# Computing 28 column blocks of the modulations on VectorE instead of 7 wide blocks on TensorE

## The chip, the cores and the metric

The program runs on one core of one Trainium2 chip. The metric is the device time of one execution in microseconds (us). The engines are PE (TensorE matmul; PEld is its weight load), DVE (VectorE), ACT (ScalarE), POOL (GpSimd) and SP (SyncE), which here issues the loads.

## What is computed

Two blocks, one behind the other, on 256 tokens of width 1024 in float32. The first block has three recurrences (HGRN2, mLSTM, SSD), three gated branches and a feed-forward with 22 pairs of hidden blocks. The second block has two layers, each with attention over the stream and a context of 256 tokens and a feed-forward. Each layer of the second block is modulated:

```
def modulation(cond, w_ada, b_ada):
    m = jax.nn.silu(cond) @ w_ada + b_ada
    return [t[..., None, :] for t in jnp.split(m, 6, axis=-1)]

for i in range(DEPTH_2):
    sh1, sc1, g1, sh2, sc2, g2 = modulation(c, w_ada[i], b_ada[i])
    csh1, csc1, cg1, csh2, csc2, cg2 = modulation(c_ctx, w_ada[i], b_ada[i])
    h = modulate(rms_norm(x, norm1_g[i]), sh1, sc1)
    ...
    x = x + g1 * (jnp.concatenate([out_a, out_b, out_c], axis=-1) @ w_out[i])
    x = x + g2 * conv_ffn(modulate(rms_norm(x, norm2_g[i]), sh2, sc2), w_up[i], conv_w[i], conv_b[i], w_down[i])
```

`w_ada[i]` is 1024 x 6144 and there are two conditions, so a layer's modulations are a product of two rows with 25 MB of weights. They don't depend on the stream, and can be computed at any time before the place that reads them: columns 0 to 2047 (shift and scale) before the layer's first norm, 2048 to 3071 (the first gate) before its output projection, 3072 to 5119 before its second norm, 5120 to 6143 (the last gate) before the end of its feed-forward.

## The kernel before, in words

Every product of the stream is done with weights on the fly. A weight tile of 128 x 1024 floats (512 KB) is loaded by SP into `raw` (four buffers), ACT casts it to a high part `wh`, DVE subtracts to get the low part `wl` (three buffers each), and PE makes three passes per 128 rows: wh with the high part of the data, wh with the low part, wl with the high part. For 256 tokens a tile is 24 matmuls of 256 columns; they write a bank `psg` (three buffers).

The modulations are made in steps that the function `ada_tick` hands out after every `pace`-th weight tile. There are two ways. `ada_pe` takes 512 columns at a time on PE: a step loads a weight tile of 256 rows x 512 columns into the same `raw`, casts and splits it like any other weight, and makes four matmuls of 512 columns with the conditions as the other operand (`psada`, L541 and L542); four steps make a wide block, and then `finish` turns its two rows into columns with four transposes (`psat`) and two small DVE additions. `ada_dve` takes 128 columns with the columns on the partitions: a 128 x 1024 tile is loaded, and for each condition one DVE instruction multiplies it with the condition's row (`ccb`, on every partition) and sums along the row (L580); a block is two steps. `ada_rows` loads and prepares `ccb` (1 MB, eight activations, eight DVE instructions).

The table `ADA` says who does which columns. Layer 0's 12 wide blocks (48 steps) all go through `ada_pe`: 36 steps during the branches of the first block, 12 in the first block's feed-forward. Layer 1's first 40 blocks of 128 columns go through `ada_dve`, in layer 0's feed-forward (the second feed-forward of the program), with tiles of their own (`araw`, three buffers); its last two wide blocks go through `ada_pe` in layer 1's attention.

Each engine executes its own list in order. A scheduler arranges these lists when the program is built: it moves instructions ahead of others where their operands allow it, so the place of a step in the code is only roughly its place in the lists. `prepare(i)` loads a layer's parameters (`plt`) and derives its small tables on DVE; it needs the columns of that layer's shift and scale.

Of the kernel before, what the change touches and what calls it, by code (L numbers as in the profile page):

```python
# [2 lines left out]

# [25 lines left out]
# columns of the modulations done on the tensor engine, 512 at a time, and on the vector engine, 128  # L29
ADA = ((range(0, 6144, 512), range(0)), (range(5120, 6144, 512), range(0, 5120, 128)))  # L30
# [3 lines left out]
# column offsets of the first block's w_in  # L34
# [4 lines left out]
# rows of the small projections: i gates, f gates, dt  # L39
# [3 lines left out]
def _ws(name, layer, c0, nk=8, r0=0):  # L43
    """[nk*128, 128] block of a weight, rows on partitions, 128 columns."""
    def cut(w):
        return w[name][layer][r0:r0 + nk * 128, c0:c0 + 128].reshape(nk, 128, 128).transpose(1, 0, 2)
    return nk * 128, cut


def _xs(name, layer, c0, half, cols=None):  # L50
    """[512, 256] block: rows on partitions, 256 columns that stream."""
# [7 lines left out]
def _ada(layer, c0, q):  # L59
    """[256, 512] block: rows on partitions, 512 columns."""  # L60
    def cut(w):
        a = w["w_ada_2"][layer][q * 256:(q + 1) * 256, c0:c0 + 512]
        return a.reshape(2, 128, 512).transpose(1, 0, 2)
    return 1024, cut


def _adat(layer, c0):
    """[1024, 128] block: columns on partitions."""
# [19 lines left out]
def _qcols(c):  # L88
    """256 columns of the window attention's queries, heads j and j + 4 side by side."""
# [35 lines left out]
def plan2(layer):  # L125
    p = [(("ada", c0, q), _ada(layer, c0, q)) for c0 in ADA[layer][0] for q in range(4)]
    p += [(("adat", c0), _adat(layer, c0)) for c0 in ADA[layer][1]]
# [21 lines left out]
def _cols(v):  # L149
    """[n*128] -> [128, n]"""  # L150
    return v.reshape(-1, 128).T


def _convc(w):
    """[K, n*128] -> [128, n*K]"""
# [121 lines left out]
class Knobs:  # L277
# [8 lines left out]
    pace3 = 5  # L286
# [13 lines left out]
def tile_two_blocks(ctx: ExitStack, tc: tile.TileContext, xT, ctxT, cst1, cst, cstw, pb1, pl0, pl1, pf0, pf1, pc, pcb, wb, w0, w1, out,  # L300
# [16 lines left out]
    class PS:  # L317
        """PSUM pools of the phase at hand"""

    def psum(**bufs):  # L320
        """Shares out the eight banks: name=number."""
# [38 lines left out]
    ones = const.tile([128, 128], F32, name="ones")  # L360
    V.memset(ones, 1.0)
    onesn = const.tile([128, 128], F32, name="onesn")
# [5 lines left out]
    def bsel(r):  # L368
        """[128, 128]: row r ones; picks and broadcasts one row."""
        return ident[:, r:r + 1].to_broadcast([128, 128])  # L370

# [21 lines left out]
    def gained(dst_h, dst_l, x, g):  # L393
        """x g, split: what the first products after a norm take; 1 / rms is applied to their results"""
# [4 lines left out]
    def mm3(o, w, rhs, nk, late=False, first=True, last=True):  # L399
        """o = W^T x in three passes; late: the low part of x comes last."""  # L400
# [11 lines left out]
    def gemm_ws(ph, key, rhs, n, nk=8, late=False, w=None):  # L412
        """out[128 features, n tokens] = W^T x; rhs(k) gives (high, low)."""
# [6 lines left out]
    def gemm_xs(ph, keys, lhs, toks, evac):  # L420
        """out[128 tokens, 256 features]; lhs(k, t) gives (high, low) of a token tile."""
# [14 lines left out]
    def rsqrt_raw(pool, a, n, tag, bufs, rows=128):  # L436
        """RS * result = 1 / sqrt(a)"""
# [3 lines left out]
        # in two halves, so that neither waits for the step before  # L441
# [13 lines left out]
    def mean_sq(x, scale=None, eps=EPS):  # L455
        """mean of squares + eps, [128 tokens, 2 blocks of them], in PSUM"""
# [20 lines left out]
    def rms_all(a):  # L477
        """[128, 256] on every partition: 1 / (RS sqrt(a)) for tokens on partitions"""
# [19 lines left out]
    # =====================================================================  # L498
    # modulation: silu(c) w + b for both conditions, features on partitions
    # =====================================================================  # L500
# [22 lines left out]
    def ada_pe(li):  # L523
        """512 columns at a time on the tensor engine; both parts of the conditions share a pass."""
# [10 lines left out]
        for c0 in ADA[li][0]:  # L535
            ps = (PS.a or PS.s).tile([128, 512], F32, tag="s", name="psada")
            for q in range(4):
# [7 lines left out]
                if q < 3:  # L545
                    yield
            rows = [Ada.rows.tile([128, 256], F32, tag="arow", name="arow", bufs=2) if Ada.rows is not None else
                    tmp.tile([128, 256], F32, tag="t256", name="arow", bufs=6) for _ in range(2)]
# [11 lines left out]
    def ada_rows(pool):  # L560
        """twice silu(c) of both conditions, on every partition"""
# [9 lines left out]
    def ada_dve(li):  # L571
        """128 columns at a time, on partitions: products summed along the rows"""
        for c0 in ADA[li][1]:
            o, sz = woff[1 + li][("adat", c0)]
            f = c0 // 128
            raw = Ada.pool.tile([128, 1024], F32, tag="araw", name="araw", bufs=Knobs.araw)
            nc.sync.dma_start(out=raw, in_=wsrc[1 + li][o:o + 128 * sz].rearrange("(p f) -> p f", p=128))
            for c in range(2):
                to = Ada.pool.tile([128, 1024], F32, tag="prod", name="prod", bufs=1) if c == 0 else raw
# [4 lines left out]
    def ada_tick():  # L584
        """After each weight tile: now and then a step."""
# [16 lines left out]
    # =====================================================================  # L602
    # convolution, SwiGLU, down projection
    # =====================================================================
    def ffn(ph, pool, halves, xh, xl, cw3, cb, causal, resid, hook=None, mid=None, raw=None):
        """halves: 1 or 2 blocks of 256 tokens. With two, the first columns take the second block first and the
# [1162 lines left out]
```

## Time and profile before

| what | value |
|---|---|
| median of 3 runs | 1767.18 us (1764.59 to 1767.67) |
| profiled execution, first to last instruction | 1767.7 us |
| PE busy | 1738.8 us (98%), PEld 1568.2 us (89%) |
| DVE busy | 1384.8 us (78%) |
| ACT busy | 983.7 us (56%) |
| loads | 273.9 MB read, 156 GB/s over the span |

The profiled execution spans 1767.7 us, which is the time of the longest of the three runs to a tenth; the median lies 0.5 us below. The busy share is an average over stages. Matmuls overlap in the pipeline, so a matmul's duration in a row is longer than what it adds to the time; the distance from one start to the next is what it adds. The stages by time: projections and HGRN2 to about 240 us, mLSTM, SSD and the branches 240 to 560, first feed-forward 560 to 760, layer 0's attention to 1000, its feed-forward 1000 to 1390, layer 1 from there.

### The profile page before, as it was taken

To read this page: it belongs to the slowest core of one execution; us is meant where nothing else is said; L and a number is where in the kernel's file an instruction comes from. 1 tells how busy PE (TensorE), PEld (TensorE's weight loads), DVE (VectorE), ACT (ScalarE), POOL (GpSimd) and SP (SyncE) were. 2 spreads that over 40 slices of the span, in tenths; PEclk is the share of its full clock that TensorE was granted. 3 is DMA by queue.
4 is the path that set the end of the run, shared out by engine and by line. 5 is a ranking of instruction groups with operands and counts; after the bars stand their busy time and mean duration, and the time that the engine had idled before them with its cause. 6 is when DMAs were issued, how large, how long until landed. Compare 5 with 4: busy or idle time off the path is not lost.

```text
span 1767.7 us, 31912 instructions
## 1 busy us (share of the span) xinstructions
PE 1738.8 (98%) x12442; PEld 1568.2 (89%) x12442; DVE 1384.8 (78%) x2716; ACT 983.7 (56%) x1723; POOL 0.2 (0%) x4
## 2 busy tenths in 40 slices
PE   7999999999999999999999999999999999999999
PEld 7999988878888999999878898888888997799999
DVE  7987967557778996877687799999656878788776
ACT  6655645445556865666676564442244556766554
POOL 0000000000000000000000000000000000000000
PEclk8999999999999999999989999999999999999999
DMA  7555445447677666654211356657433543046564
GB/s 233 159 154 152 138 132 157 147 126 222 218 228 228 187 190 221 209 170 139 86 67 47 105 163 189 183 171 232 129 96 107 168 132 120 24 141 195 174 196 132
DMA packets 80502, 276.97 MB, mean 157 GB/s; under 512 B 9056, under 2 KB 13792, under 8 KB 80224
## 3 DMA queue, kind: packets, MB, share of 16 engines
q1 hardware_dynamic: 80352, 274.94, 49.8%
q8 instruction: 98, 1.61, 0.4%
q14 instruction: 52, 0.43, 0.1%
HBM read 273.86 MB, written 1.05 MB: 156 GB/s over the span
## 4 chain that ended last, share of the span: by engine, by line
PE 51%; DVE 3%; ACT 1%; issue 0%; ACTq 0%
PE psg L404 12%; PE psg L407 12%; PE psg L406 11%; PE pso L1574 3%; PE psx L429 2%; PE psx L431 2%; PE psx L430 2%; PE psp L1562 2%; PE psc L1517 1%; PE psc L1519 1%; PE psc L1518 1%; DVE wl L385 0%; ACT Pp L1529 0%; DVE mx L1523 0%; PE psc L1521 0%
## 5 line engine op out<-in xcount | busy, mean ns | idle before, releaser
L383 ACT CAST wh<-raw 128x1024 fp32r<-128x1024 f32 (+1 forms) x475 | 490.9, 1037 | 531.0 <-PE psg L406 423.7
L385 DVE TENSOR_TENSOR wl<-raw,wh 128x1024 fp32r<-128x1024 f32 (+1 forms) x475 | 572.5, 1208 | 206.8 <-ACT wh L383 203.2
L404 PE MATMUL psg<-XH,wh 128*128 128x256 f32 (+1 forms) x1288 | 400.7, 314 | 3.6 <-ACT XH L390 1.9
L407 PE MATMUL psg<-XH,wl 128*128 128x256 f32 (+1 forms) x1288 | 398.8, 312 | 0.3 <-DVE wl L385 0.3
L406 PE MATMUL psg<-XL,wh 128*128 128x256 f32 (+1 forms) x1240 | 387.5, 313 | 0.7 <-DVE XL L1304 0.5
L404 PEld LDWEIGHTS psg<-XH,wh 128*128 128x128 f32 x1288 | 243.0, 189 | 22.0 <-ACT XH L390 2.3
L407 PEld LDWEIGHTS psg<-XH,wl 128*128 128x128 f32 x1288 | 243.3, 189 | 15.9 <-DVE wl L385 1.0
L406 PEld LDWEIGHTS psg<-XL,wh 128*128 128x128 f32 x1240 | 234.5, 189 | 16.1 <-DVE XL L1304 1.1
L404 PE MATMUL psg<-xh,wh 128*128 128x256 f32 x704 | 203.4, 289 | 1.8 <-ACT xh L390 1.3
L406 PE MATMUL psg<-xl,wh 128*128 128x256 f32 x704 | 200.5, 285 | 0.9 <-DVE xl L391 0.9
L407 PE MATMUL psg<-xh,wl 128*128 128x256 f32 x704 | 200.1, 284 | 0.3 <-DVE wl L385 0.3
L404 PE MATMUL psg<-hh,wh 128*128 128x256 f32 (+1 forms) x592 | 179.6, 305 | 0.1
L407 PE MATMUL psg<-hh,wl 128*128 128x256 f32 (+1 forms) x592 | 178.5, 302 | 0.0
L406 PE MATMUL psg<-hl,wh 128*128 128x256 f32 (+1 forms) x592 | 178.5, 302 | 0.0
L404 PEld LDWEIGHTS psg<-xh,wh 128*128 128x128 f32 x704 | 134.9, 192 | 6.0 <-ACT xh L390 1.5
L406 PEld LDWEIGHTS psg<-xl,wh 128*128 128x128 f32 x704 | 135.1, 192 | 2.9 <-DVE xl L391 1.4
L407 PEld LDWEIGHTS psg<-xh,wl 128*128 128x128 f32 x704 | 134.9, 192 | 2.2 <-issue 1.3
L406 PEld LDWEIGHTS psg<-hl,wh 128*128 128x128 f32 x592 | 111.5, 188 | 5.3 <-DVE hl L391 0.2
L404 PEld LDWEIGHTS psg<-hh,wh 128*128 128x128 f32 x592 | 110.9, 188 | 5.9 <-ACT hh L390 0.6
L407 PEld LDWEIGHTS psg<-hh,wl 128*128 128x128 f32 x592 | 111.2, 188 | 5.5
L429 PE MATMUL psx<-wh,XH 128*128 128x256 f32 x384 | 110.0, 287 | 1.1 <-DVE ss L1379 0.5
L430 PE MATMUL psx<-wh,XL 128*128 128x256 f32 x384 | 108.5, 283 | 0.0
(435 smaller groups left out, 3237.8 us busy)
## 6 DMA issues: line engine op xcount, KB each, us to landing
raw<-w SPq DMA_DIRECT2D x254, 512.0 KB, 3.7
raw<-wb SPq DMA_DIRECT2D x197, 512.0 KB, 4.3
araw<-w SPq DMA_DIRECT2D x40, 512.0 KB, 4.2
raw<-w SPq DMA_DIRECT2D x16, 384.0 KB, 3.4
raw<-wb SPq DMA_DIRECT2D x8, 384.0 KB, 3.2
xres<-xT SPq DMA_DIRECT2D x16, 128.0 KB, 3.6
plt<-pl SPq DMA_DIRECT2D x2, 588.0 KB, 5.5
xres<-ctxT SPq DMA_DIRECT2D x8, 128.0 KB, 2.7
```

Of the source, the lines that this page charges most:

```text
L383: S.copy(wh[:, 0:sz], raw[:, 0:sz])
L385: V.tensor_tensor(wl[:, 0:sz], raw[:, 0:sz], wh[:, 0:sz], ALU.subtract)
L404: T.matmul(o, wh[:, k], xh, start=(first and k == 0), stop=False)
L406: T.matmul(o, wh[:, k], xl, start=False, stop=False)
L407: T.matmul(o, wl[:, k], xh, start=False, stop=(last and not late and k == nk - 1))
L429: T.matmul(o, xh, wh[:, k % 4], start=(k == 0), stop=False)
L430: T.matmul(o, xl, wh[:, k % 4], start=False, stop=False)
L431: T.matmul(o, xh, wl[:, k % 4], start=False, stop=(k == 7))
L1517: T.matmul(o, qh, kh, start=True, stop=False)
L1518: T.matmul(o, qh, kl, start=False, stop=False)
L1562: T.transpose(ps[:, b], p[:, b * 128:(b + 1) * 128], ident)
L1574: T.matmul(po[:, i % 4], pt[:, b], v, start=(b == 0), stop=(b == nb - 1))
```

## The change

28 of layer 0's 48 column blocks of 128 go from `ada_pe` to `ada_dve`. Columns 0 to 2559 (20 blocks, `e` = 0) are handed out from the branches on, with tiles from the weights' own four `raw` buffers (`own` false). Columns 2560 to 5119 (5 wide blocks) stay on PE, behind the 20. Columns 5120 to 6143 (8 blocks, `e` = 2) go in front of layer 1's 40 in the second feed-forward, with tiles `araw`. A second `ccb` is loaded and prepared early in the first block. `pace3`, the pace in the first feed-forward, is 3 instead of 5. The first of the two products of a block is written in bfloat16 (`prod`; only the sum is used), and `prod`'s buffer also holds the rows of `finish`. Two small constants shrink, comments are taken out. In the second feed-forward `prepare(1)` comes two hidden blocks later, behind a line that makes sure that 48 steps are done.

```
-ADA = ((range(0, 6144, 512), range(0)), (range(5120, 6144, 512), range(0, 5120, 128)))
+ADA = ((range(0, 2560, 128), range(2560, 5120, 512), range(5120, 6144, 128)),
+       (range(0), range(5120, 6144, 512), range(0, 5120, 128)))
...
-    pace3 = 5
+    pace3 = 3
...
-            rows = [Ada.rows.tile([128, 256], F32, tag="arow", name="arow", bufs=2) if Ada.rows is not None else
-                    tmp.tile([128, 256], F32, tag="t256", name="arow", bufs=6) for _ in range(2)]
+            if Ada.rows is not None:
+                row = Ada.rows.tile([128, 512], F32, tag="prod", name="arow", bufs=1)
+                rows = [row[:, 0:256], row[:, 256:512]]
+            else:
+                rows = [tmp.tile([128, 256], F32, tag="t256", name="arow", bufs=6) for _ in range(2)]
...
-    def ada_dve(li):
+    def ada_dve(li, e, own):
-        for c0 in ADA[li][1]:
+        for c0 in ADA[li][e]:
...
+            if own:
+                o, sz = woff[1 + li][("adat", c0)]
+                raw = Ada.pool.tile([128, 1024], F32, tag="araw", name="araw", bufs=Knobs.araw)
+                nc.sync.dma_start(out=raw, in_=wsrc[1 + li][o:o + 128 * sz].rearrange("(p f) -> p f", p=128))
+            else:
+                raw = weight_raw(1 + li, ("adat", c0))
             for c in range(2):
-                to = Ada.pool.tile([128, 1024], F32, tag="prod", name="prod", bufs=1) if c == 0 else raw
+                to = Ada.pool.tile([128, 1024], BF16, tag="prod", name="prod", bufs=1) if c == 0 else raw
...
     ada_prep()
-    Ada.pace, Ada.steps, Ada.rows = Knobs.pace0, ada_pe(0), p1
+    Ada.pool, Ada.cb = p1, ada_rows(p1)
+    Ada.pace, Ada.steps, Ada.rows = Knobs.pace0, chain(ada_dve(0, 0, False), ada_pe(0)), p1
...
-        ada_steps(max(0, 17 - Ada.done))
+        ada_steps(max(0, 32 - Ada.done))
...
-            Ada.pace, Ada.steps = Knobs.pace2, ada_dve(1)
+            Ada.pace, Ada.steps, Ada.done = Knobs.pace2, chain(ada_dve(0, 2, True), ada_dve(1, 2, True)), 0
 
             def hook(j):
-                if j == 16:
+                if j == 13:
+                    ada_steps(max(0, 16 - Ada.done))
+                if j == 18:
+                    ada_steps(max(0, 48 - Ada.done))
                     LS[1] = prepare(1)
```

The lists of the engines show where the steps fall. First DVE in the branches of the first block, before the change: `wl` is the split of a weight tile, two of the branch's for each of the modulation's, `th` and `mixed` are the branch's own work, `mod0` the end of a wide block.

```order
L385 TENSOR_TENSOR wl_5198<-raw_5194,wh_5196 128x1024
L385 TENSOR_TENSOR wl_5231<-raw_5227,wh_5229 128x1024
L385 TENSOR_TENSOR wl_5263<-raw_5259,wh_5261 128x1024
L1173 SCALAR_TENSOR_TENSOR th_5036<-th_5036,psg_5200 128x256
L1174 TENSOR_TENSOR mixed_603<-mixed_603,th_5036 128x256
L385 TENSOR_TENSOR wl_5282<-raw_5278,wh_5280 128x1024
L385 TENSOR_TENSOR wl_5315<-raw_5311,wh_5313 128x1024
L530 TENSOR_TENSOR mod0_93<-psat_5269,pf0_575 128x8
L385 TENSOR_TENSOR wl_5346<-raw_5342,wh_5344 128x1024
L532 TENSOR_TENSOR mod0_93<-mod0_93,psat_5269 128x8
```

The same place with the change; L590 is the product with its sum (on `prod` for the first condition, on `raw` itself for the second) and the reading of the sum.

```order
L389 TENSOR_TENSOR wl_5091<-raw_5087,wh_5089 128x1024
L1184 SCALAR_TENSOR_TENSOR th_4878<-th_4878,psg_5023 128x256
L1185 TENSOR_TENSOR mixed_629<-mixed_629,th_4878 128x256
L389 TENSOR_TENSOR wl_5124<-raw_5120,wh_5122 128x1024
L590 ISA prod_5220,mod0_93<-raw_5218,ccb_585,pf0_575 128x1024
L590 ISA mod0_93 128x1
L389 TENSOR_TENSOR wl_5158<-raw_5154,wh_5156 128x1024
L590 ISA raw_5218,mod0_93<-raw_5218,ccb_585,pf0_575 128x1024
L590 ISA mod0_93 128x1
L1184 SCALAR_TENSOR_TENSOR th_4948<-th_4948,psg_5093 128x256
L1185 TENSOR_TENSOR mixed_629<-mixed_629,th_4948 128x256
L389 TENSOR_TENSOR wl_5191<-raw_5187,wh_5189 128x1024
```

One split in three is gone; for every four weight tiles two products have come. The tile `raw_5218` is loaded into the buffer that `raw_5087` leaves, so its load starts when `wl_5091` is made, and one more split lies between the two.

The load queue of SP at this place, before the change (`w0` are layer 0's modulations, `wb` the first block's weights).

```order
L376 DMA raw_5893<-w0 128x1024
L376 DMA raw_5909<-wb 128x1024
L376 DMA raw_5942<-wb 128x1024
L376 DMA raw_5974<-w0 128x1024
L376 DMA raw_5993<-wb 128x1024
```

And with the change.

```order
L380 DMA raw_5081<-w0 128x1024
L380 DMA raw_5087<-wb 128x1024
L380 DMA raw_5120<-wb 128x1024
L380 DMA raw_5154<-wb 128x1024
L380 DMA raw_5187<-wb 128x1024
L380 DMA raw_5218<-w0 128x1024
```

Every fifth load is now the modulation's, where it was every third. Of the 20 blocks, 19 stand in DVE's list between the start of the branches and the first feed-forward's first products, the last one a little behind; the 20 steps of `ada_pe` that are left all stand in the first feed-forward or directly behind it.

## Rows read from the trace of the kernel before

**Rows 1.** The page: span, and busy time of two engines.

```profile
span 1767.7 us, 31912 instructions
...
PE 1738.8 (98%) x12442; PEld 1568.2 (89%) x12442; DVE 1384.8 (78%) x2716; ACT 983.7 (56%) x1723; POOL 0.2 (0%) x4
```

**Rows 2.** Busy time by stretch: PE, PEld, DVE, ACT, POOL; granted clock, DMA share, GB/s.

```profile
20.00:100.00 80.00, 76.40 (x612) 74.27 (x611) 69.58 (x136) 54.32 (x91) 0.00 (x0) 0.96 0.56 173
240.00:560.00 320.00, 317.91 (x2299) 270.99 (x2298) 220.44 (x366) 170.14 (x305) 0.00 (x0) 0.99 0.58 181
560.00:600.00 40.00, 35.88 (x283) 33.40 (x283) 36.17 (x89) 27.90 (x50) 0.00 (x0) 1.00 0.62 191
1040.00:1240.00 200.00, 200.00 (x900) 163.56 (x900) 194.50 (x293) 77.96 (x107) 0.00 (x0) 1.00 0.60 185
1240.00:1360.00 120.00, 120.00 (x528) 97.11 (x527) 70.73 (x91) 42.92 (x53) 0.00 (x0) 1.00 0.34 105
```

**Rows 3.** Waits of PE from 240 to 560 us: in total, times, longest.

```profile
PE psada L541 <- ACT wh L383: 1.6, 1, 1.6
```

**Rows 4.** Waits of ACT from 405 to 560 us.

```profile
ACT wh L383 <- PE psg L406: 43.8, 29, 3.5
```

**Rows 5.** Waits of ACT from 1040 to 1240 us.

```profile
ACT wh L383 <- PE psg L406: 103.2, 31, 4.6
```

**Rows 6.** Matmuls of tile psada alone, by stretch: PE busy (count), PEld, ACT.

```profile
240.00:560.00 320.00, 39.82 (x144) 11.98 (x144) 5.52 (x18) 0.99 0.58 181
560.00:600.00 40.00, 2.36 (x8) 0.67 (x8) 0.00 (x0) 1.00 0.62 191
```

**Rows 7.** Timeline of PE around two steps: start, duration, what.

```profile
298.40 0.39 PE L541 MATMUL psada<-wh,ccr 128*4 128x512 f32 x1
...
299.42 0.41 PE L528 MATMUL psat<-ct,arow 4*128 4x4 f32 x4
299.76 0.38 PE L404 MATMUL psg<-xh,wh 128*128 128x256 f32 x1
...
305.47 0.40 PE L541 MATMUL psada<-wh,ccr 128*4 128x512 f32 x1
...
306.40 0.28 PE L404 MATMUL psg<-yh,wh 128*128 128x256 f32 x1
306.52 0.28 PE L406 MATMUL psg<-yl,wh 128*128 128x256 f32 x1
```

**Rows 8.** Timeline of PE at the first feed-forward's start.

```profile
567.24 0.71 PE L482 MATMUL psr<-ct,rcy 128*128 128x128 f32 x4 [1.79 <-DVE rcy L451]
567.88 0.41 PE L528 MATMUL psat<-ct,arow 4*128 4x4 f32 x4
...
582.69 0.40 PE L541 MATMUL psada<-wh,ccr 128*4 128x512 f32 x1
```

**Rows 9.** Timeline of DVE in the same place.

```profile
566.85 0.17 DVE L1248 TENSOR_SCALAR g5n1g<-plt 128x8 f32<-128x8 f32 x1 [2.44 <-DMA plt<-pl]
```

**Rows 10.** Line L580, the product with its sum, and the reading of the sum.

```profile
L580 DVE DVE_READ_ACCUMULATOR2_ANT mod<- x80: 80/83/88, 1046.6 to 1253.6; 128x1 f32 x80
L580 DVE CUSTOM_DVE_ANT_0 prod<-araw,ccb,pf x40: 1273/1278/1283, 1045.4 to 1251.0; 128x1024 f32<-128x1024 f32 x40
```

**Rows 11.** The page's groups: cast and split of weight tiles (busy, mean ns, idle before).

```profile
L383 ACT CAST wh<-raw 128x1024 fp32r<-128x1024 f32 (+1 forms) x475 | 490.9, 1037 | 531.0 <-PE psg L406 423.7
L385 DVE TENSOR_TENSOR wl<-raw,wh 128x1024 fp32r<-128x1024 f32 (+1 forms) x475 | 572.5, 1208 | 206.8 <-ACT wh L383 203.2
```

**Rows 12.** The page's DMA issues: count, size, median us to landing.

```profile
raw<-w SPq DMA_DIRECT2D x254, 512.0 KB, 3.7
```

**Rows 13.** Tile ccb, its DVE instructions.

```profile
L568 DVE SCALAR_TENSOR_TENSOR ccb<-th,ccb x8: 421/422/424, 1041.9 to 1045.1; 128x256 f32<-128x256 f32 x8
```

**Rows 14.** Timeline of SP, 0 to 70 us: start, duration, loads issued.

```profile
21.94 4.26 SPq L494 DMA_DIRECT2D xres<-xT  x8
31.85 17.34 SPq L376 DMA_DIRECT2D raw<-wb  x8
```

More of the change, by code (lines that the diff above doesn't have):

```diff
@@ L2 @@
 from contextlib import ExitStack
+from itertools import chain
 import numpy as np
@@ L125, in plan2 @@
 def plan2(layer):
-    p = [(("ada", c0, q), _ada(layer, c0, q)) for c0 in ADA[layer][0] for q in range(4)]
-    p += [(("adat", c0), _adat(layer, c0)) for c0 in ADA[layer][1]]
+    p = [(("ada", c0, q), _ada(layer, c0, q)) for c0 in ADA[layer][1] for q in range(4)]
+    p += [(("adat", c0), _adat(layer, c0)) for e in (0, 2) for c0 in ADA[layer][e]]
     for h in range(2):
@@ L317, in tile_two_blocks @@
     class PS:
+        pass
     def psum(**bufs):
@@ L359, in tile_two_blocks @@
     ident = C("ident")
-    ones = const.tile([128, 128], F32, name="ones")
+    ones = const.tile([128, 1], F32, name="ones")
     V.memset(ones, 1.0)
-    onesn = const.tile([128, 128], F32, name="onesn")
+    onesn = const.tile([128, 1], F32, name="onesn")
     V.memset(onesn, 1.0 / 1024.0)
@@ L534, in ada_pe @@
         last = None
-        for c0 in ADA[li][0]:
+        for c0 in ADA[li][1]:
             ps = (PS.a or PS.s).tile([128, 512], F32, tag="s", name="psada")
@@ L569, in ada_rows @@
         return t
-    def ada_dve(li):
-        for c0 in ADA[li][1]:
-            o, sz = woff[1 + li][("adat", c0)]
+    def ada_dve(li, e, own):
+        for c0 in ADA[li][e]:
             f = c0 // 128
-            raw = Ada.pool.tile([128, 1024], F32, tag="araw", name="araw", bufs=Knobs.araw)
-            nc.sync.dma_start(out=raw, in_=wsrc[1 + li][o:o + 128 * sz].rearrange("(p f) -> p f", p=128))
+            if own:
[4 more added lines that the diff above has]
+                raw = weight_raw(1 + li, ("adat", c0))
             for c in range(2):
-                to = Ada.pool.tile([128, 1024], F32, tag="prod", name="prod", bufs=1) if c == 0 else raw
+                to = Ada.pool.tile([128, 1024], BF16, tag="prod", name="prod", bufs=1) if c == 0 else raw
                 V.tensor_tensor_reduce(to, raw, Ada.cb[:, c], 0.5, Ada.pf[li]("bada")[:, f:f + 1], ALU.mult, ALU.add,
```

## The prediction

> **What bounds the kernel now.** I read the page first: PE is busy 98% of a span of 1767.7 us, DVE 78% [rows 1]. A share of busy time can mislead, so I went to the stretches in which the change works [rows 2] and asked who waits for whom there. From 240 to 560 us, where 36 of layer 0's 48 modulation steps lie (144 matmuls, four a step [rows 6]), PE is busy 317.9 of 320 us and DVE 220.4; the longest wait of PE in all of it is 1.6 us [rows 3]. The preparation of the weights is the other way round: ACT's casts wait for PE to give a buffer back, 43.8 us in the last 155 us of the stretch [rows 4], and over the whole program 423.7 us [rows 11]. So the weights are ready before PE wants them, and PE alone sets the pace. The one stretch near the change where that fails is the start of the first feed-forward, 560 to 600 us: PE idles 4.1 us [rows 2], 1.8 us of it in front of the norm's broadcast [rows 8], behind a DVE that itself stood 2.4 us for a load of parameters [rows 9].
>
> **What a step on PE is worth.** The timeline gives the distance of starts, which is what counts: a plain step goes from 305.47 to the next weight's first matmul at 306.40, 0.93 us; a step with the transposes of `finish` from 298.40 to 299.76, 1.36 us, so `finish` adds 0.43 us [rows 7]. The four matmuls thus start 0.23 us apart, though each lasts 0.4 us in its row. The Trainium skill ("TensorE: Matmul & The Clock Gate", Back-to-back issue gap) states about 131 ns per matmul of 512 columns in a sustained stream, and 216 ns alone; by the first of these a step would be an estimated 0.52 us and the sum 11 us smaller. The rows show a stream, and neither figure; the trace decides.
>
> **The change, part by part.**
>
> Taken from PE: 7 of 12 wide blocks, 28 steps and 7 finishes: 28 x 0.93 + 7 x 0.43 = 26.0 + 3.0 = 29.0 us. In place it is more movement than that: 36 steps leave 240 to 560 us, and the first feed-forward has 20 steps instead of 12. Not all of it is on the path: two of the old steps (8 matmuls [rows 6]) and one finish (567.88 [rows 8]) lie in the 40 us in which PE idles anyway, and filled holes: 2 x 0.93 + 0.43 = 2.3 us off. That leaves 26.7 us.
>
> Put on DVE: 56 products of 1.28 us and 56 readings of 0.08 us [rows 10], against 28 splits of 1.21 us [rows 11] that go. One product has a bfloat16 output, which no row shows; half of 1.28 us is the floor if the written bytes decided, 1.28 us the ceiling by the nearest row, with the same two float32 inputs; I take 1.28. In the branches, 19 of the 20 blocks come to 19 x 2 x 1.36 = 51.7 us and 36 splits go (43.6 us), so DVE rises from 220.4 us to some 228 us, of the 283 us that the stretch has left when 36 steps and 8 finishes are gone from it (36.9 us). It stays under PE: price 0, while the cover holds.
>
> The wait that this adds: a product needs its tile, whose load starts when a buffer of the weights' ring comes free, one split ahead of it in DVE's list. A load takes 3.7 us [rows 12], and PE goes through a weight tile of 24 matmuls in about 2.8 us (0.12 us from start to start, 306.40 to 306.52 [rows 7]), so DVE will stand about 1 us at the first product. Queued behind it are the next weight's split and the evacuation of the branch's products; PE waits for the first, and through its result buffers for the second. The two products and the wait come to some 3.7 us in which DVE also owes one split; with three buffers the preparation runs up to two tiles (5.6 us) ahead, so most of these stalls end in that lead. Bounds: 0, and 20 blocks x 2.7 us = 54 us if every pair of products stood bare. I take 1 us in all, close to the lower end, because DVE has 55 us of slack there.
>
> The start of the program: a second `ccb` costs 8 DVE instructions of 0.42 us [rows 13], 3.4 us, in a stretch where DVE is busy 69.6 of 80 us and PE already idles 3.6 us [rows 2]. The 1 MB load itself falls into a hole of SP: its issues end at 26 us and the next weight's starts at 31.85 us [rows 14]. Bounds 0 and 3.4 us; I take 1 us, because DVE has 10 us of slack but little lead.
>
> The first feed-forward's start: in DVE's list one pair of products now lies around the last sums of squares, and the parameters' small tables are spread through the norm's chain of short instructions; the standstill of 2.4 us for the parameters [rows 9] is covered by more work ahead of it. Gain up to 2.4 us, loss up to two products, 2.7 us. I take 0.
>
> The second feed-forward: 16 more products and readings, 16 x 1.36 = 21.8 us of DVE, which is busy 194.5 of 200 us from 1040 to 1240 us. PE is busy 200.0 of 200 there all the same, and ACT's casts wait for PE 103.2 us [rows 5]: DVE is full and still ahead. The products come no denser than before, they only end later, and from 1240 to 1360 us DVE has 49 us free [rows 2]. Price 0; without that cover 21.8 us. `prepare(1)` two hidden blocks later moves inside the same cover. The later steps of `ada_pe` in the first feed-forward are counted above: they cost 0.93 us each, wherever PE is full.
>
> Sum: -26.7 + 1 + 1 = -24.7 us, 1767.7 - 24.7 = 1743.0 us for an execution like the profiled one. The median of the runs lies 0.5 us under it: **1742.5 us**.
>
> **Rivals.**
>
> *Part is given back on DVE.* If the ring of four buffers or the products in front of the branches' work expose some 0.5 us for each of 20 blocks, and the start costs its whole 3.4 us, the change gives back 10 to 13 us: about 1752. For it: every stall sits in front of a split; DVE's use there rises from 69% to 81%. Against it: the casts' waits for PE [rows 4].
>
> *PE isn't the bound.* PE's busy time is a sum of overlapping, partly modelled durations, and PEld is busy only 271 of the 320 us [rows 2]. If what really paces the branches were loads or casts, the removed steps would only make room for waits, and the time would stay near 1766. The Trainium skill ("Perfetto Trace Analysis", Identifying the Most-Contended Engine) warns just so: matmul occupancy is no good measure of the distance to the limit, the share of weight loads is. Against it stands the unbroken row of starts through the steps [rows 7] and that one wait of 1.6 us [rows 3].
>
> *Slower: a block as a brake on the weights.* The modulation's tile keeps its ring buffer until its second product is done, and only then can the weight four places on be loaded (3.7 us), cast (1.04 us) and split (1.21 us): 6.0 us in all, against 2.8 us that PE needs for a tile. Bare, that is 3.2 us for each of 20 blocks, 64 us, and a time near 1806. It decides from 1.5 us a block on: then 30 us eat the 26.7 us and 3.5 us more. Against it: the next three tiles are in other buffers, and the lead would have to be gone before.
>
> **How the numbers follow.** The forecast, 1737 to 1748: 0.66. Part given back, 1748 to 1764: 0.20. PE not the bound, within 0.2% (3.5 us, about what a measurement of this kernel can tell from no change): 0.06. Slower through the ring: 0.05. Better than 1737, if the first feed-forward's start also loses its standstill and every step counts (29.0 + 1.6 + 2.4 us: down to 1734): 0.03. The range 1735 to 1756 leaves out the two that end elsewhere and the worse half of the second case, some 0.2 in all. Faster 0.89, same 0.06, slower 0.05.
>
> **What the next profile would show.** Right: 112 matmuls of `psada` fewer, none before the first feed-forward; PE as full from 240 us as before, and the branches ending some 36 us earlier (36.9 less the stalls), of which the first feed-forward gives back about 10 (8 x 0.93 + 0.43 for what it does more, 2.3 for the filled holes); DVE near 81% busy in the branches; waits of DVE for loads there of about 1 us, some 20 times, and hardly any of PE; the second feed-forward as long as before. Wrong: waits of PE for `wl` or `wh` in the branches, by the dozen; PE idle for more than 5 us from 20 to 100 us, or for more than 8 us around the first feed-forward's start; or PE's starts further apart between 1040 and 1360 us.

## The result, and the profile after

The changed kernel takes 1748.74 us (median of 4 runs, 1745.11 to 1749.94); beside it the kernel before takes 1767.43 us (4 runs, 1764.59 to 1768.96). The ratio is 0.9897, with an interval of 0.9879 to 0.9915: faster, as forecast, and inside the range, but 6.2 us above the 1742.5 us named. It lies 0.7 us outside the band of 1737 to 1748 us that the prediction gave to its own case, in the band of its first rival; the traces show that it isn't that rival's mechanism that put it there.

The page of the changed kernel answers to [rows 1].

```profile
span 1746.6 us, 31615 instructions
...
PE 1707.4 (98%) x12302; PEld 1552.8 (89%) x12302; DVE 1415.7 (81%) x2794; ACT 957.2 (55%) x1689; POOL 0.2 (0%) x4
```

PE has 31 us less, DVE 31 us more, and PE's share is 98% again. The next lines are busy time by stretch (columns as in [rows 2]) of the program's start, the branches, the first feed-forward's start and the second feed-forward, to be set against [rows 2].

```profile
20.00:100.00 80.00, 73.27 (x602) 71.51 (x602) 71.95 (x143) 56.09 (x98) 0.00 (x0) 0.99 0.58 180
240.00:525.00 285.00, 281.59 (x2123) 256.15 (x2122) 214.29 (x380) 131.25 (x249) 0.00 (x0) 0.99 0.55 172
525.00:565.00 40.00, 33.56 (x265) 32.75 (x263) 36.51 (x93) 26.47 (x49) 0.00 (x0) 0.96 0.51 162
1020.00:1220.00 200.00, 200.00 (x906) 163.80 (x906) 194.55 (x294) 78.16 (x108) 0.00 (x0) 1.00 0.60 183
```

The matmuls of `psada` alone, by stretch [rows 6]: none is left in the branches, 72 stand in the first feed-forward and 8 behind it.

```profile
240.00:525.00 285.00, 0.00 (x0) 0.00 (x0) 0.00 (x0) 0.99 0.55 172
525.00:746.00 221.00, 19.55 (x72) 6.05 (x72) 2.46 (x8) 0.99 0.67 208
746.00:764.00 18.00, 2.02 (x8) 0.68 (x8) 0.61 (x2) 1.00 0.55 181
```

PE is still full in the branches (281.6 of 285 us) and in the second feed-forward (200.0 of 200), with DVE at 75% in the one and 97% in the other. PE's idle time has grown at the start (6.7 of 80 us, 3.6 before [rows 2]) and at the first feed-forward's start (6.4 of 40 us).

Where the time went shows when the same matmul starts in the two traces:

| matmul | before, us | after, us | after less before |
|---|---|---|---|
| first `psl` (HGRN2) | 55.14 | 56.61 | +1.47 |
| first `psF` (mLSTM) | 242.09 | 244.21 | +2.12 |
| first `psw` (mLSTM) | 246.21 | 249.47 | +3.26 |
| last product on `mh` (end of the branches) | 560.18 | 527.34 | -32.84 |
| first product on `XH` (first feed-forward) | 572.92 | 539.74 | -33.18 |
| last product on `hh` there | 769.60 | 746.82 | -22.78 |
| 120th `psx` (layer 0's projections) | 787.46 | 769.33 | -18.13 |
| first product on `hh` of the second feed-forward | 1189.05 | 1170.48 | -18.57 |
| last one of its first pass | 1267.23 | 1248.64 | -18.59 |
| end | 1767.7 | 1746.6 | -21.1 |

Each column is one execution. The first 260 matmuls of PE are the same in all kernels, yet the 261st starts between 46.8 and 50.3 us in the twelve traces of this document, at 49.95 us in the kernel before and at 50.28 us here; so 0.3 us of the first rows is not the change's.

From the first `psF` to the last product on `mh` both kernels make the same 1727 matmuls into `psg`, and the kernel before 36 steps and 8 finishes more. This stretch takes 283.1 us instead of 318.1: the branches give 35.0 us. The first feed-forward takes back 10.4, and another 4.7 us go where nothing was expected, between the last product of the first feed-forward and layer 0's projections. The waits of PE in the branches, 240 to 525 us, come to 3.4 us (engine, line, waited for; total, times, longest):

```profile
PE psr L1143 <- DVE rqy L455: 1.5, 1, 1.5
PE psg L410 <- DVE ml L395: 1.0, 2, 0.7
PE psg L408 <- ACT mh L394: 0.7, 1, 0.7
PE psg L411 <- DVE wl L389: 0.2, 1, 0.2
```

The products themselves, line L590 (ns min/median/max, first and last start, forms), and what DVE waited for before them (us, times):

```profile
L590 DVE CUSTOM_DVE_ANT_0 prod<-raw,ccb,pf x20: 1267/1284/1286, 235.6 to 557.6; 128x1024 bf16<-128x1024 f32 x20
L590 DVE CUSTOM_DVE_ANT_0 raw<-raw,ccb,pf x20: 1264/1280/1286, 236.9 to 563.6; 128x1024 f32<-128x1024 f32 x20
...
  DMA raw<-w: 21.5, 14
```

A bfloat16 output changes nothing (1284 against 1280 ns). DVE stands 14 times for a tile, 1.5 us on average. Only 0.2 us of PE's waiting is for a split (`wl`), but the longest wait, 1.5 us for `rqy`, comes behind two products in a norm of the branches, the first of which stood 2.56 us for its tile:

```profile
452.75 1.28 DVE L590 CUSTOM_DVE_ANT_0 prod<-raw,ccb,pf 128x1024 bf16<-128x1024 f32 x1 [2.56 <-DMA raw<-w]
...
453.96 0.41 DVE L1124 TENSOR_SCALAR ms<-psn 4x256 f32<-4x256 f32 x1
454.29 1.26 DVE L590 CUSTOM_DVE_ANT_0 raw<-raw,ccb,pf 128x1024 f32<-128x1024 f32 x1
...
455.50 0.34 DVE L448 TENSOR_SCALAR rqy<-ms 4x128 int32<-4x128 int32 x2
```

In the kernel before `rqy` starts 0.45 us behind `ms` (473.84 and 474.29 us), here 1.54 us, and PE doesn't wait for it there.

**The turn.** The lists of ACT, DVE and PE where the first feed-forward ends (start, duration, instruction, idle time before it and its releaser):

```profile
749.13 0.61 ACT L557 COPY arow<-psada 4x256 f32<-4x256 f32 x2
749.65 2.50 ACT L465 ACTIVATE sq<-xres,pb1t 128x256 f32<-128x256 f32 x6
752.06 2.92 ACT L387 CAST wh<-raw 128x1024 fp32r<-128x1024 f32 x3
```

```profile
747.13 0.42 DVE L1327 TENSOR_TENSOR xres<-psg,xres 128x256 f32<-128x256 f32 x1 [0.27 <-PE psg L411]
...
756.11 1.23 DVE L389 TENSOR_TENSOR wl<-raw,wh 128x1024 fp32r<-128x1024 f32 x1
757.26 0.15 DVE L455 SCALAR_TENSOR_TENSOR rcy<-rct,rcy 128x2 f32<-128x2 f32 x1
757.33 1.22 DVE L389 TENSOR_TENSOR wl<-raw,wh 128x1024 fp32r<-128x1024 f32 x1
758.46 0.15 DVE L451 TENSOR_TENSOR rct<-rcy 128x2 f32<-128x2 f32 x1
758.53 1.22 DVE L389 TENSOR_TENSOR wl<-raw,wh 128x1024 fp32r<-128x1024 f32 x1
...
762.18 1.27 DVE L1313 SCALAR_TENSOR_TENSOR h<-xres,gx,rr 128x256 f32<-128x256 f32 x3
```

```profile
748.56 0.40 PE L546 MATMUL psada<-wl,ccr 128*2 128x512 f32 x1
...
757.39 0.39 PE L435 MATMUL psx<-wl,XH 128*128 128x256 f32 x1 [1.48 <-DVE wl L389]
```

The last two steps of `ada_pe` are handed out behind the feed-forward, and PE makes them from 746.94 us on. They leave layer 0 one weight tile ahead; the next three casts then lie behind the squares of the norm and the copies of `arow` on ACT, come all at once at 752.06, and their three splits stand between the norm's tiny instructions. From the last residual (747.13) to the first `h` (762.18) it is 15.05 us. In the kernel before it was 10.3 us:

```profile
769.92 0.42 DVE L1316 TENSOR_TENSOR xres<-psg,xres 128x256 f32<-128x256 f32 x1 [0.23 <-PE psg L407]
...
780.24 0.88 DVE L1302 SCALAR_TENSOR_TENSOR h<-xres,gx,rr 128x256 f32<-128x256 f32 x2
```

**The first feed-forward's start.** PE there, by the timeline:

```profile
539.74 0.73 PE L408 MATMUL psg<-XH,wh 128*128 128x256 f32 x3 [2.92 <-ACT XH L394]
540.79 0.41 PE L408 MATMUL psg<-XH,wh 128*128 128x256 f32 x1
541.43 0.41 PE L408 MATMUL psg<-XH,wh 128*128 128x256 f32 x1
```

And busy time and clock behind it, by stretch:

```profile
539.70:543.50 3.80, 3.76 (x18) 3.72 (x19) 3.80 (x12) 2.28 (x7) 0.00 (x0) 0.55 0.31 113
543.50:550.00 6.50, 6.50 (x56) 6.42 (x54) 5.11 (x19) 4.95 (x10) 0.00 (x0) 1.00 0.00 0
```

Behind the norm's broadcast PE is now empty for 2.9 us; before, a `finish` [rows 8] and the rest of a product stood there, and the wait was 1.9 us. For 3.8 us after it the granted clock is 0.55, nearly all of it the lower of the two levels (1.2 instead of 2.4 GHz): starts 0.21 us apart instead of 0.12. Before, the granted clock was 1.00 in the same place [rows 2]. That doesn't make the fall the change's alone: in the run with the second feed-forward's part alone (below), PE's wait for `XH` is 1.86 us, as in the kernel before, and there the clock fell all the same:

```profile
569.31:573.22 3.91, 3.91 (x18) 3.76 (x19) 3.91 (x12) 2.75 (x8) 0.00 (x0) 0.56 0.24 96
```

A little later PE waits 1.9 us for `ag` (551.98 us), where the kernel before doesn't wait.

### The profile page after: what moved, and what is told of

It is laid out like the page before. It is cut to its first block, busy times and chain, and to the rows that moved or that the text cites. A ratio compares the mean times of both kernels' runs of the same rounds, so it can differ in the third digit from the quotient of the medians.

```text
span 1746.6 us, 31615 instructions
## 1 busy us (share of the span) xinstructions
PE 1707.4 (98%) x12302; PEld 1552.8 (89%) x12302; DVE 1415.7 (81%) x2794; ACT 957.2 (55%) x1689; POOL 0.2 (0%) x4
## 4 chain that ended last, share of the span: by engine, by line
PE 50%; DVE 4%; ACT 1%; DMA 1%; issue 1%; ACTq 0%; DVEq 0%; SPq 0%
PE psg L408 12%; PE psg L411 12%; PE psg L410 11%; PE pso L1585 2%; PE psx L433 2%; PE psx L435 2%; PE psx L434 2%; PE psp L1573 1%; PE psc L1528 1%; DVE wl L389 1%; PE psc L1530 1%; DVE mx L1534 1%; PE psc L1529 1%; ACT Pp L1540 0%; ACT wh L387 0%
## 5 line engine op out<-in xcount | busy, mean ns | idle before, releaser
L387 ACT CAST wh<-raw 128x1024 fp32r<-128x1024 f32 (+1 forms) x447 | 462.1, 1037 | 506.0 <-PE psg L410 413.2
L389 DVE TENSOR_TENSOR wl<-raw,wh 128x1024 fp32r<-128x1024 f32 (+1 forms) x447 | 538.3, 1207 | 151.2 <-ACT wh L387 148.7
L435 PE MATMUL psx<-wl,XH 128*128 128x256 f32 x384 | 108.1, 283 | 1.5 <-DVE wl L389 1.5
```

The source lines that it names most:

```text
L387: S.copy(wh[:, 0:sz], raw[:, 0:sz])
L389: V.tensor_tensor(wl[:, 0:sz], raw[:, 0:sz], wh[:, 0:sz], ALU.subtract)
L435: T.matmul(o, xh, wl[:, k % 4], start=False, stop=(k == 7))
```

## The experiments

Ten runs follow, nine of them of new kernels. The ratio is to the kernel before, run on the same chip. The last column is worked out from each trace: from the start of the first feed-forward's last product on `hh` to the start of the 120th `psx`.

| run | median, us | ratio, interval | turn, us |
|---|---|---|---|
| kernel before (profile) | 1767.43 | 1 | 17.85 |
| changed kernel (profile) | 1748.74 | 0.9897 [0.9879, 0.9915] | 22.51 |
| e0_again | 1749.51 | 0.9905 [0.9887, 0.9922] | 25.12 |
| e1_end | 1747.21 | 0.9895 [0.9876, 0.9915] | 17.84 |
| e2_pace2 | 1746.19 | 0.9890 [0.9869, 0.9910] | 17.86 |
| e4_ccblate | 1746.28 | 0.9894 [0.9874, 0.9913] | 25.00 |
| e3_ff2only | 1756.80 | 0.9955 [0.9941, 0.9970] | 17.84 |
| e5_double | 1753.68 | 0.9931 [0.9918, 0.9944] | 23.76 |
| e7_both | 1745.47 | 0.9882 [0.9867, 0.9897] | 17.86 |
| e8_hole | 1742.58 | 0.9862 [0.9846, 0.9879] | 17.86 |
| e6_ff1dve | 1759.55 | 0.9958 [0.9944, 0.9973] | 17.85 |
| e9_more | 1741.36 | 0.9854 [0.9831, 0.9878] | 17.86 |

The medians of the kernel before lie between 1766.06 and 1767.47 us in the four comparisons, but single executions of one program lie 4 to 10 us apart. So edits worth 1 to 4 us are judged by their stretch of the trace, and the time only for the sum of several.

**The changed kernel again.**

> The changed kernel once more, so that the next three are compared with it on the same chip. 1746 to 1751 us; the ratio to the kernel before 0.988 to 0.991.

1749.51 us, as expected. Its trace has the same waits at the turn (1.5 us for `wl`, 0.5 us for `sacc`), but behind them the clock fell too: granted 0.91 from 746 to 785 us, 1.00 in the first execution over its turn. So the turn costs 4.7 us in one execution and 7.3 us in another, over the 17.85 us without steps at the end.

**The last steps earlier.**

```
     def resid1(m, ps, c, last):
         V.tensor_tensor(x[:, m], ps, x[:, m], ALU.add)
+        if last and m == 3:
+            ada_rest()
```

> The changed kernel, but the last steps of ada_pe run after the fourth of the last eight products of the first feed-forward instead of behind it. Theory (the two steps at the very end hold the cast, split and buffers that layer 0's first projections need, and so lay the norm's chain bare): the 4.6 us that are lost from the end of the first feed-forward to layer 0's first projections come back, 3.5 to 4.6 us, so 1744 to 1745.5 us; the norm's chain takes some 10 to 11 us instead of 15. Rival (the turn is longer because the norm's chain itself fell in another place between the splits): at most 1 us, 1748 or more.

The norm's chain is as short as before, 10.31 us (749.17 to 759.48 us), and the turn 17.84 us. So the theory holds for the place: the two steps at the end, and nothing else, made it long; every run without steps there has a turn of 17.84 to 17.86 us. The size on the whole is not shown: 1747.21 us is 2.3 us under the changed kernel's median beside it, short of the 4 us expected, and the two intervals overlap. Part was paid at once: three steps and a finish now stand together, and behind them PE waits for a cast.

```profile
736.91 0.39 PE L408 MATMUL psg<-hh,wh 128*128 128x256 f32 x1 [0.80 <-ACT wh L387]
```

**A closer pace in the first feed-forward.**

```
-    pace3 = 3
+    pace3 = 2
```

> The changed kernel with a pace of 2 instead of 3 in the first feed-forward: the 20 steps of ada_pe stand closer, and none is left at the end. Theory as for the run with the last steps earlier: 1744 to 1745.5 us. Rival (the beginning of the first feed-forward, where DVE is busy 36 of 40 us, has no room for steps that stand closer): the gain at the end is paid back by waits of PE for wl from 540 to 640 us, 2 us or more, and the time is 1747 us or more.

Both theory and rival came true, each in its place. The turn is 17.86 us. At the other end the 20th block now lies in the norm's chain on DVE, where its first product stands 2.4 us for its tile (535.26 us), and PE waits for it; from 525 to 600 us:

```profile
PE psr L486 <- DVE rcy L455: 3.0, 1, 3.0
PE psg L408 <- ACT XH L394: 2.3, 1, 2.3
```

The first of these is 0.6 us in the changed kernel. From 536 to 552 us the granted clock is 0.68. 1746.19 us, 3.3 us under the changed kernel beside it.

**The second `ccb` later.**

```
-    Ada.pool, Ada.cb = p1, ada_rows(p1)
+    Ada.pool = p1
...
             silu2(mq[:, j * 256:(j + 1) * 256], conv4(ps, P("mcw"), P("mcb"), j))
             yield
+        Ada.cb = ada_rows(p1)
         for c in range(4):
             gemm_xs(0, [("mv", c, 0), ("mv", c, 1)], lhs, (0, 1),
```

> The changed kernel with the second ccb loaded and prepared later, in the middle of the projections (ahead of the mLSTM's values) instead of at 55 us. Theory (the 8 tanh and 8 DVE instructions are in the way of the first projections; they cost 1.5 to 2 us there): PE's offset to the kernel before at 60 to 240 us falls from 1.3 to 2.1 us to under 0.6, and the time is 1746.5 to 1747.5 us. Rival (the loss comes from the order that the scheduler makes of everything else): the offset stays, 1748.5 us.

The wait of PE in front of the first `psl` falls from 1.43 us in the changed kernel (first line) to 0.25 us (second):

```profile
56.61 1.16 PE L854 MATMUL psl<-hq,hk 128*128 128x128 f32 x8 [1.43 <-DVE hq L822]
```

```profile
52.66 1.16 PE L854 MATMUL psl<-hq,hk 128*128 128x128 f32 x8 [0.25 <-DVE hq L822]
```

Nothing takes its place: against the kernel before, PE's starts stay put from 50 to 160 us (2.43, then 2.48 us earlier), where the changed kernel falls back from 0.34 to 1.34 us later. So the `ccb` costs 1.2 us where the change puts it, and nothing in the middle of the projections. In the time it can't be seen (1746.28 us, 3.2 us under its neighbour, which it didn't earn there alone).

**The second feed-forward's part alone.**

```
(on the kernel before)
-ADA = ((range(0, 6144, 512), range(0)), ...
+ADA = ((range(0, 5120, 512), range(5120, 6144, 128)), ...
...
-            Ada.pace, Ada.steps = Knobs.pace2, ada_dve(1)
+            Ada.pace, Ada.steps, Ada.done = Knobs.pace2, chain(ada_dve(0), ada_dve(1)), 0
```

> The kernel before, with one part of the change alone: the 8 blocks of the last gate (2 wide blocks, 8 steps and 2 finishes) go from TensorE to VectorE in the second feed-forward. Theory (the cover of the second feed-forward holds, price 0): 8 x 0.93 + 2 x 0.43 = 8.3 us less than the kernel before, a ratio of 0.9953, and PE as full from 1040 to 1360 us. Rival (DVE is the limit there and 21.8 us of products show in part): a ratio of 0.998 or more, with waits of PE for wl in the second feed-forward.

`prepare(1)` comes two hidden blocks later here too, as in the change. 0.9955 against 0.9953 expected. In its trace PE runs 2.83 us ahead of the kernel before at 400 us and 10.77 us at 800 us: 7.94 us come from the 8 steps and 2 finishes that leave the first feed-forward (8.3 us by the sum). In the second feed-forward it gives back 0.6 us of it, though DVE has 21.8 us more to do there.

**DVE's slack in the branches.**

```
             for c in range(2):
-                V.tensor_tensor_reduce(to, raw, Ada.cb[:, c], ...
+                for _ in range(2 if c == 0 and not own else 1):
+                    V.tensor_tensor_reduce(to, raw, Ada.cb[:, c], ...
```

> The changed kernel with the first of the two products of each of the 20 early blocks made twice: 20 x 1.36 = 27 us more of DVE in the branches, nothing else. Theory (DVE has some 55 us of slack there and PE sets the pace): at most 3 us more than the changed kernel, 1749 to 1752 us. Rival (DVE is already nearly the limit of the branches, part is given back there): 10 us or more on top, 1759 us or more, with waits of PE for wl in the branches.

1753.68 us, 4.2 us over the changed kernel's second median: more than the theory's 3, far from the rival's 10. PE's waits for `wl` from 240 to 530 us come to 2.1 us for 27 us of additional work, so the branches themselves have the slack. Some 2.5 us are paid at the first feed-forward's start (14.9 us from the last product on `mh` to the first on `XH`, 12.2 and 12.4 in the two traces of the changed kernel), where the 19th block's products stand in the norm's chain; from 520 to 566 us:

```profile
PE psr L486 <- DVE rcy L455: 3.3, 1, 3.3
PE psg L408 <- ACT XH L394: 2.3, 1, 2.3
```

**Everything on DVE in the first feed-forward.**

```
-ADA = ((range(0, 2560, 128), range(2560, 5120, 512), range(5120, 6144, 128)),
+ADA = ((range(0, 5120, 128), range(0), range(5120, 6144, 128)),
...
-    pace3 = 3
+    pace3 = 1
```

> The changed kernel with the 5 wide blocks of the first feed-forward also on VectorE: 20 more blocks of 128 columns there, with a pace of 1, and no ada_pe left in layer 0. PE is rid of 20 x 0.93 + 5 x 0.43 = 20.8 us; DVE gets 40 x 1.36 = 54.4 us in place of 20 splits (24.4 us), 30 us more in a feed-forward of some 185 us where it is busy 36 of 40 us in the first 100. Theory (DVE has no room in the first half of the feed-forward, where a pace of 1 puts the products): it becomes the limit there, PE waits for wl by the dozen, and less than half of the 20.8 us is gained, 1739 to 1749 us. Rival (PE sets the pace there as everywhere else): the whole 20.8 us and the turn's 4 us, 1724 to 1728 us.

1759.55 us: 20.8 us are taken from PE, and the time rises by 10. The theory named the cause, but not the size. Busy time by stretch (columns as above):

```profile
560.00:600.00 40.00, 33.08 (x260) 31.02 (x258) 38.11 (x69) 19.65 (x33) 0.00 (x0) 1.00 0.70 210
600.00:640.00 40.00, 31.78 (x215) 30.00 (x216) 34.86 (x87) 20.95 (x34) 0.00 (x0) 0.87 0.54 170
```

PE's waits from 540 to 760 us:

```profile
PE psg L411 <- DVE wl L389: 12.8, 19, 1.8
PE psg L408 <- ACT wh L387: 6.5, 7, 2.1
```

PE idles 15 of these 80 us, waits for `wl` 19 times, and its granted clock falls to 0.87. These are waits "for `wl` or `wh`, by the dozen", which the forecast named as a sign of being wrong, and they show what the change itself avoids: the same products that cost little at 75% of DVE cost more than they save at 90%.

**Both small edits.**

```
     def hook1(j):
+        if j == 13:
+            Ada.pace = 2
```

with `ccb` prepared later, as above.

> The changed kernel with ccb prepared later (in the middle of the projections) and the pace in the first feed-forward 3 until its 14th pair of hidden blocks and 2 from there, so that no step is left at the end and the beginning is as before. Theory: 1.2 us from the start and 4 to 6 us from the turn to layer 0's projections: 1742 to 1745 us, a ratio of 0.986 to 0.988. Rival (steps that stand closer cost as much in the second half of the feed-forward as at its end): 1747 us or more.

1745.47 us, half a microsecond above the range expected: the turn is 17.86 us, and the start as in the run with `ccb` alone. In its trace the clock fell twice at the first feed-forward's start (granted 0.82 from 536 to 552 us).

**The hole filled.**

```
-ADA = ((range(0, 2560, 128), range(2560, 5120, 512), range(5120, 6144, 128)),
+ADA = ((range(0, 2304, 128), range(2560, 5120, 512), range(5120, 6144, 128), range(2304, 2560, 128)),
...
-    ... chain(ada_dve(0, 0, False), ada_pe(0)), p1
+    ... chain(ada_dve(0, 0, False), ada_pe(0), ada_dve(0, 3, False)), p1
```

on top of the run before. The edit does two things: it puts a step of `ada_pe` into the hole, and it takes the last two early blocks, whose products stood in the norm's chain and just behind it, away from there (they come at 695 to 713 us).

> As the run with both edits, but the last 2 of the 20 early blocks come behind the 20 steps of ada_pe, so that a step of ada_pe stands in the hole of PE at the first feed-forward's start, where PE now waits 2.9 us for the normed stream and then runs at a lower granted clock for some 4 us. Theory: the step fills the hole, 0.9 us, and if the clock stays up 1.8 us more: 1740 to 1744 us. Rival (its cast and split stand in the norm's own chain and lengthen the wait): no gain against the run with both edits, or 1 to 2 us more.

1742.58 us, ratio 0.9862. PE at the first feed-forward's start:

```profile
532.87 0.40 PE L545 MATMUL psada<-wh,ccr 128*4 128x512 f32 x1
533.10 0.39 PE L546 MATMUL psada<-wl,ccr 128*2 128x512 f32 x1
...
534.89 0.50 PE L408 MATMUL psg<-XH,wh 128*128 128x256 f32 x2 [0.94 <-ACT XH L394]
```

And busy time of as many products behind it, in this run (first line) and in the run before (second):

```profile
534.90:547.10 12.20, 10.32 (x73) 9.10 (x74) 12.20 (x26) 10.22 (x22) 0.00 (x0) 1.00 0.27 85
536.03:548.20 12.17, 10.34 (x72) 10.16 (x73) 10.85 (x35) 9.17 (x19) 0.00 (x0) 0.86 0.22 68
```

The step fills the hole, the wait is 0.94 us instead of 2.92, and the granted clock stays at 1.00. From the last product on `mh` to the first on `XH` it is 9.55 us instead of 11.98, with the step in it: that is the gain, and the step and the shorter chain share in it. Of the 1.8 us that the theory gave to the clock nothing shows: 73 products take 12.20 us at 1.00 and 72 take 12.17 us at 0.86. In this run DVE, which makes the low parts of the normed stream, is busy all of that time, and PE waits 1.0 us for a `wl`. The interval (to 0.9879) ends where that of the changed kernel's first comparison begins, so this version beats both kernels; from the run before (0.9867 to 0.9897) the time alone doesn't tell it apart.

**One wide block more.**

```
+ADA = ((range(0, 2304, 128), range(3072, 5120, 512), range(5120, 6144, 128), range(2304, 3072, 128)),
```

on top of the run before.

> As the run with the hole filled, but one wide block more goes from TensorE to VectorE: 4 wide blocks stay, and 6 column blocks come behind them, in the second half of the first feed-forward, where DVE is busy 25.6 of 40 and 56 of 65 us. Theory (there is room for the 6 us that DVE gets on balance): 4 x 0.93 + 0.43 = 4.2 us less than the run with the hole filled, a ratio of 0.983 to 0.985. Rival (the products stand in front of the products of the feed-forward's end): no gain, 0.986 or more.

1741.36 us, 0.9854: between theory and rival, and not to be told from the run before (the profiled spans are 1736.3 and 1736.5 us). In its trace PE is 2.0 us further ahead at the end of the first feed-forward, half of the 4.2 us. Behind it the lead is lost: 1.1 us go around 880 us, where its granted clock is 0.94 from 860 to 940 us and that of the other run 0.96. The clock falls there in every trace, for longer or shorter (0.87 from 870 to 935 us with `ccb` later, 0.89 in the kernel before, 0.95 in the run before this one), so this part is spread and not the edit. The rest goes in steps of 0.3 us in the second feed-forward, where no wait differs; its cause is open, and so is why only half of the 4.2 us came.

## Why the prediction was right, point by point

**PE is the bound: right.** 28 steps and 7 finishes went, and the time followed. From the first `psF` to the end of the branches it is 35.0 us less, against the 36.9 us less some 1 us of stalls that the forecast named; PE idles 3.4 us there, 2.1 us before. The second feed-forward's part alone gave 7.94 us for 8.3, which agrees within 5% with the 0.93 us of a step and the 0.43 us of `finish` [rows 7], read as distances of starts. The prediction's remark that the rows show neither of the two figures it cites for a matmul of 512 columns is too strong: the rows' 0.23 us lies within 7% of the second. So the rival that PE isn't the bound is refuted. The Trainium skill ("Perfetto Trace Analysis", Identifying the Most-Contended Engine) warns that matmul busy time is no good measure of how near a kernel is to its limit; the trace agrees so far as PE's busy share is 98% in both kernels and doesn't tell them apart. The rival of the ring as a brake isn't seen either: from 225 to 562 us ACT waits for a load of the branches' weights (`wb`) three times, 1.4 us in all.

**Stalls of DVE in the branches: right in kind, too small in size.** Forecast 1 us in all. The loads make DVE stand 14 times, 1.5 us on average; PE idles 1.3 us more than before in a stretch without the 36 steps, and the longest wait, the 1.5 us for `rqy`, comes of two products in a norm. DVE is busy 75% there and not the 81% forecast: 17 of the 20 blocks, and not 19, lie between 240 and 525 us.

One place looks worse than it is, the mLSTM's chain of tiny instructions, where a product now stands between two of them (starts 1.55 us apart, 0.44 before). The first `psw` comes 1.1 us later behind `psF`. But PE isn't idle there (28.00 of 28 us busy from 242 to 270 us): its list has 36 matmuls of the branch's weights between the two, where 24 and two of a step stood. In the second execution of the changed kernel PE waits 0.4 us there.

**The start: right in the sum, though a sign of being wrong came.** Forecast 1 us with bounds of 0 and 3.4; the second `ccb` costs 1.2 us. PE idles 6.7 us from 20 to 100 us (6.8 in the second execution), over the 5 us that the forecast named as a sign; with `ccb` later it is 3.5. Against the kernel before its starts fall back by only 1.0 us from 50 to 160 us, since that one's clock was lower (0.83 from 20 to 40 us, here 0.97) and PE was busy for longer with the same work. Until `psF` another 0.8 us go in small steps, and some 0.7 with `ccb` later too; their cause is open.

**The second feed-forward: right.** No change from 1189 to 1267 us. ACT's waits for PE there are 103.2 us in 31, exactly as before [rows 5].

**The first feed-forward's start: partly wrong.** I took 0. PE's order keeps pace up to the first product on `XH` (-32.84 to -33.18 us). From there to the last product on `hh` it is 10.4 us more, where 7 steps and one finish more are worth 6.9 us. Of the other 3.5 us, 1.9 us is the wait for `ag`, which I had not seen and whose cause isn't followed here. The lower clock, 3.8 us with starts 0.21 us apart instead of 0.12, is worth up to 1.7 us, which no bound of mine had. Between the two traces of one program that differ in it, the kernel before and the run with the second feed-forward's part alone, it cost 0.8 us (the 73rd product behind the wait starts 9.5 us behind the first in the one and 10.3 us in the other). The run with the hole filled shows no gain where the clock stays up, so what it costs the changed kernel isn't shown. The Trainium skill ("TensorE: Matmul & The Clock Gate", Part 1: The HAM clock gate) says that the throttled clock is the default and activity releases it; the trace agrees so far: granted 0.55 behind the empty 2.9 us, and 1.00 again behind 3.8 us in which PE was busy.

**The step that failed** is "the later steps of `ada_pe` in the first feed-forward are counted above: they cost 0.93 us each, wherever PE is full". 18 of the 20 do. The last two, with their finish, were handed out behind the feed-forward, and there the turn took 4.7 to 7.3 us more where 2 x 0.93 + 0.43 = 2.3 us were counted: 2.4 to 5.0 us lost, gone in every kernel that ends its steps earlier. The section on the change already said that these steps stand "in the first feed-forward or directly behind it"; I priced their number and not their place.

**The sum.** Forecast -24.7 us, measured -18.7 us in the medians and -21.1 us in the two profiled spans. The 2.4 us between these two are the choice of the execution: the reported time lies some 2 us over the span (1751.39 us for a span of 1749.6), so the profiled execution of the kernel before counts as some 1769.7 us, above its median, and that of the changed kernel, 1748.47 us, lies at its median.

Of the 3.6 us that are missing in the spans, the turn is 2.4 (4.7 for 2.3), the stretch from `mh` to the turn 2.2 (10.1 where the forecast's 10.2 less the turn's 2.3 make 7.9), the start 1.1 (2.1 for 1) and the branches 0.9 (35.0 for 35.9). Against them the stages behind the turn are 3.0 us faster after than before in these two traces. 0.9 us of that recurs: the second pass over `hh` in the second feed-forward takes 46.7 us in all ten traces with the change and 47.7 us in the two without; its cause stays open. The rest is no more than the spread of executions: from the 120th `psx` to the end the twelve traces take 975.2 to 980.2 us, the kernel before the longest of them, and the changed kernel 977.3 and 977.2.

**The last half microsecond** was luck. I took the profiled span for the reported time and the profiled execution for a typical one. The first is some 2 us too low, and the second some 2.3 us too slow; the two errors nearly cancel, and so the kernel before's median, 1767.43 us, does lie 0.3 us under the span.

## What to carry to other kernels

Work that moves to an engine with slack is free only where it doesn't stand in a chain of short, dependent instructions: the same product cost PE next to nothing between the weight tiles of the branches and 1 to 3 us in a norm. The last pieces of background work belong ahead of the last stretch that covers them, not behind it, because there they take the weights' lead from the next stage. And a hole in the bounding engine is worth filling with background work, for the time itself; in two traces the clock then stayed up as well, but that gains only where the engine behind the hole isn't held up by another.

## What the runs showed of the hardware

The spread of several microseconds between executions of one program goes for the most part with the mean granted clock of TensorE: one kernel (`ccb` later) ran 1752.03 us at 0.988 and 1744.57 us at 0.993. It isn't all: of the five executions with the doubled products the slowest, 1756.37 us, has the highest clock, 0.993. The low stretches stand behind the same few idle places, but not in each execution: at the turn the clock fell in the second profile of the changed kernel and not in the first, with the same waits ahead of it, and at the first feed-forward's start, behind the same wait of 1.86 us, it fell in one of two traces. Behind a wait of 2.3 to 2.9 us there it fell in all eight, behind 0.94 us in neither of two.
